# Layer A's tail in a two-layer decoder step on one core: which queue position the reload casts, the last head's output chain and a mixing of rows get

## The chip, the core and the metric

One core of a Trainium2 chip runs the whole step. The time is device microseconds of that core; smaller is better. TensorE does the matmuls, VectorE (DVE), ScalarE (ACT) and GpSimd (POOL) the elementwise work, and SyncE (SP) issues the DMAs.

## The reference

The input is 1024 prompt tokens and 8 sample tokens, 1032 columns in all, with model width 1024 and inner width 2048. Layer A is a gated linear recurrence in 8 heads, layer B a causal spatial gating unit. Both end in the same way:

```python
o = rmsnorm(o, g_norm).reshape(B, L, D_INNER)      # layer A, per head
y = (o * silu(z)) @ w_out
h = h + y
gate = sigmoid(rmsnorm(h, norm_ple[i]) @ w_ple_gate[i])
h = h + gate * (p[i] @ w_ple_proj[i])
```

The change touches the last head of layer A, the start of `w_out` in layer A, and one step of `w_out` in both layers.

## The kernel before, in words

**Layout.** Activations lie feature-major: 128 features on the partitions, tokens along the free dimension. The columns are cut into three groups c = 0, 1, 2 of 384, 384 and 264. A float32 product is made of three matmuls on rounded parts: `hi` is a ScalarE cast to the fast format, `lo` a DVE subtraction of what the cast lost (helper `split`; `bh`/`bl` are such pairs for activations, `whi`/`wlo` for weights).

**Order.** TensorE's program order is written out by hand: a tick counter runs small generators between the matmul groups, and each generator yields the number of ticks that it waits. The other engines' order is set by a scheduler from priorities (`tc.high_priority`), from `tc.issue_after(x)` (not ahead of x) and from when the code issues the work. At run time each engine works through its row strictly in order, so an instruction that waits holds up all that stands behind it. All DMAs here go through SP's one row.

**End of layer A.** For the last head (h = 7), `head_proj` makes the projections f, q, v and at last z (function `zz`, in the order c = 2, 0, 1). `recur` then works through eight tiles of 128 tokens: `pd` and `po` in PSUM, a state update on DVE (`S`), `out_sum` on ScalarE (a copy `on<-po`, then a square that sums). `finish` scales `on`, waits some ticks, transposes it on TensorE into `pt_o` (one buffer with the tag "pt"), and DVE multiplies it with z into `oz`, which is spilled to the DRAM tensor `ozd`. Beside this, `reload` brings the finished heads of `ozd` back as the `w_out` operand: for c = 0 through `zstg`, for c = 1 through three buffers `f`, row by row (DMA `f<-ozd`, cast `bh<-f`, subtraction `bl<-f,bh`). A buffer can be loaded again only when its subtraction is done.

**`last_fill`.** Between the last heads' steps TensorE runs twelve blocks of the per-layer embedding product (`pple`, PSUM tile `ps_pple`, three banks, each freed by a ScalarE copy to `pple_t`). Then come the first `w_out` products `ps_o`, which for c = 0 and 1 start before the loop over heads is drained. Rows of c = 2 are reloaded by `zstg<-ozd` into tiles that hold the `pple` operand until then (`bh_138`).

**`w_out`.** `out_phase` uses a seven-product form with sums of rows (`t1` to `t4`; function `unit`). It loads sums and residual rows (`raw<-d0t`, `h<-d0t`, `h<-in_xT`), and mixes two more sets of four rows for the second half: `quarters` loads them, `mix_rows` makes four DVE subtractions (`raw<-raw`), `store_sums` stores them. The hooks of `unit` (numbers after each product) say where that is issued. `exchange` reloads the results for the second half in the last unit of the first half.

Of the kernel before, what the change touches and what calls it, by code (L numbers as in the profile page):

```python
# [12 lines left out]
AF = mybir.ActivationFunctionType  # L13
# [12 lines left out]
NH = 8  # L26
# [4 lines left out]
PRI = 400  # L31
NWARM = 12
ZQ = 7
ZR = 3
# [7 lines left out]
W = (384, 384, 264)  # L42
# [38 lines left out]
def trunk_kernel(ctx, tc, xT, st, pT, nrm, wina, lbl, gna, wouta, winb, lng, lnb, lngr, lnbr,  # L81
# [3 lines left out]
    V, A, G, PE = nc.vector, nc.scalar, nc.gpsimd, nc.tensor  # L85
# [134 lines left out]
    last, rest = {}, {}  # L220
# [118 lines left out]
    def pple(l, ph, pl, half, place):  # L339

        wh, wl = take("p", l, half)
        for c in CH:
            for mm in range(4):
                ps = pp.tile([P, 512], F32, name="ps_pple", tag="mm", bufs=3)
                for k in range(2):
                    b = 2 * mm + k
                    mm3(ps[:, :W[c]], blk(wh, b), blk(wl, b), ph[c][:, k, :], pl[c][:, k, :], k == 0, k == 1)
                t = place(c, mm)
                with tc.high_priority(offset=PRI if l else 0):
                    last["pple"] = A.copy(t, ps[:, :W[c]])  # L350
                nc.sync.dma_start(ppd[l][4 * half + mm][:, OFF[c]:OFF[c] + W[c]], t)
                yield 1

# [1 line left out]
        nc.sync.dma_start(stg, src)  # L355
        split(hi, lo, stg)

    def load_zt(zt, parts, stage, n=2, lag=0, tie=True):


        todo = [(ozd[c][:, k0 + k:k0 + k + n, :], *(x[:, k:k + n, :] for x in zt[c, k0][:2]), W[c])
                for c, k0 in parts for k in range(0, zt[c, k0][2], n)]
        return load_list(todo, stage, lag, tie)

    def load_list(todo, stage, lag=0, tie=True, behind=False):

        stg = []
        def fetch(i):
            if i < len(todo):
                stg.append(stage(todo[i][3]))  # L370
                last["zt"] = nc.sync.dma_start(stg[i], todo[i][0])

        for i in range(len(todo) + lag):
            if not lag:
                fetch(i)
            if i >= lag:
                _, zh, zl, _ = todo[i - lag]
                with tc.issue_after(rest["u2"].ins) if behind else ExitStack():
                    hi = A.copy(zh, stg[i - lag])
                if tie:  # L380
                    tc.keep_in_program_order(hi)
                with tc.issue_after(rest["sum"].ins) if behind else ExitStack():
                    V.tensor_tensor(zl, stg[i - lag], zh.bitcast(F32), ALU.subtract)

            if lag:
                fetch(i)
            yield
# [258 lines left out]
    def z_gate(out, src, m, w, sg=None):  # L646
        sg = sg or fq.tile([P, 384], F32, name="sg", bufs=2)
        last["read"] = A.activation(sg[:, :w], src, AF.Sigmoid)
        V.scalar_tensor_tensor(sg[:, :w] if out is None else out, src, gn16[:, m:m + 1], sg[:, :w], ALU.mult, ALU.mult)
        return sg  # L650
# [46 lines left out]
    def head_proj(h, r):  # L697

        r["t0"] = tk.now
        if h:  # L700
            wt = take("a", 8 + h)
            for c in CH:
                fk(h, r, wt, c)
            wt = take("a", h)
            for c in CH:
                qq(h, r, wt, c)
                tk.spawn(decay(h, r, c), DEC[c])
        else:
            for c in CH:
                tk.spawn(decay(h, r, c), (1, 8, 18)[c])  # L710
        r["vs"] = wa.tile([NS, DV], F32, name="vs", bufs=1)
        tk.spawn(sample(h, r), 1)
        tk.spawn(recur(h, r), 1)
        for m in range(2):
            wt = take("a", 16 + 2 * h + m)
            for c in CH:
                w = W[c]
                ps = proj(wt, hh[c], hl[c], c)
                vf = wa.tile([P, 384], F32, name="vf", bufs=2)
                with tc.high_priority(offset=PRI):  # L720
                    last["read"] = A.copy(vf[:, :w], ps[:, :w])
                tk.spawn(v_token_major(h, r, m, c, vf), 3)
                tk.tick()
        if h < NH - 1:
            return

        def zz(wt, m, c):
            if not m:
                r["zs"][c] = wa.tile([P, 2, W[c]], F32, name=f"zs{c}")
            ps = proj(wt, hh[c], hl[c], c)  # L730
            z_gate(r["zs"][c][:, m, :], ps[:, :W[c]], m, W[c])
            tk.tick()
            if m == 1:
                r[f"z{c}"] = True

        wz, wz1 = take("a", 32 + 2 * h), take("a", 33 + 2 * h)
        zt.update(new_zt())
        for c in (2, 0, 1):
            zz(wz, 0, c)
            zz(wz1, 1, c)  # L740
            if c == 2:
                for cc in (0, 1):
                    tk.spawn(reload(r, cc))
                r["p"] = p_in_act(0, lambda w: wa.tile([P, 384], F32, name="vf", bufs=2)[:, :w])

    def reload(r, c):

        yield lambda: not any(p[2].__name__ == "mix_more" for p in tk.procs)
        lag = 2 + c
        gen = load_zt(zt, [(c, 0)], (stage2(wa, 2), one(lambda: fq.tile([P, 384], F32, name="f", bufs=3)))[c],  # L750
                      2 - c, lag, False)
        for _ in range(lag):
            next(gen)
        yield lambda: r.get(f"z{c}")
        for _ in gen:
            yield 1

    def v_token_major(h, r, m, c, vf):
        if not m:
# [122 lines left out]
    def out_sum(po, ss):  # L882

        on = wa.tile([P, DV], F32, name="on", bufs=6)
        with tc.high_priority(offset=PRI):
            A.copy(on, po)
            A.activation(po, po, AF.Square, accum_out=ss)
        return on

    def out_scale(ss, n):  # L890
# [45 lines left out]
    def finish(h, r, c, ss, ons):  # L936

        n = NT[c]
        if h < NH - 1:
            r["zs"][c] = wa.tile([P, 2, W[c]], F32, name=f"zs{c}")  # L940
            nc.sync.dma_start(r["zs"][c], zd[h][c])
            r[f"z{c}"] = True
        y = out_scale(ss[:, :n], n)
        yield 2
        with tc.issue_after(last["read"].ins):
            for i in range(n):
                A.activation(ons[i], ons[i], AF.Copy, scale=y[:, i:i + 1])
        yield (3, 3, 7)[c]
        yield lambda: r.get(f"z{c}") and slot(r, 2)
        oz = r["oz"][c] = wa.tile([P, 2, 384], F32, name="oz", bufs=2)  # L950
        for i in range(n):
            pt = out_transpose(ons[i], "pt")
            with tc.high_priority(offset=PRI):
                V.tensor_tensor(oz[:, :, i * P:(i + 1) * P], pt, r["zs"][c][:, :, i * P:(i + 1) * P], ALU.mult)
            yield 4 if i < n - 1 else 1
        if c < 2:
            spill(h, r, c)
            spilled.add((h, c))
# [69 lines left out]
    zt = {}  # L1028
    spilled = set()
    fine[0] = True  # L1030
    for h in range(NH):
# [5 lines left out]
        r = new_head() if h else r0  # L1037
# [52 lines left out]
    def out_phase(key, b, ssq, first, done, pre, begin):  # L1090
# [3 lines left out]
        with ExitStack() as s:  # L1094
# [117 lines left out]
            gen = [None]  # L1212
# [7 lines left out]
            def rows_of(m):  # L1220
                def go():
                    for i in (2, 3):
                        load_h(m + i)
                return go

            def exchange():

                assert next(mixer, None) is None
                o = dict(b)
                for n, to in (("b11", "b11"), ("b21", "t2"), ("b12", "b21"), ("b22", "t1"),  # L1230
                              ("t2", "t3"), ("t1", "b22"), ("t3", "t4"), ("t4", "b21")):
                    b[n] = o[to]
                todo = quarter("b11") + quarter("b21") + quarter("b12") + quarter("b22")
                todo += [(ozd[2][:, 8 + k, :], b["c2"][0][:, k, :], b["c2"][1][:, k, :], W[2]) for k in range(8)]
                todo += quarter("t2") + quarter("t1") + quarter("t3") + quarter("t4")
                turns = itertools.cycle([zr] * ZR + [lambda w: raw()[:, :w]] * 4)
                gen[0] = load_list(todo, lambda w: next(turns)(w), ZR + 4, False, True)
                steps(gen[0], ZR + 4)()

            def last_exchange():  # L1240
# [2 lines left out]
                steps(gen[0], ZR)()  # L1243

            units(0, range(2, KT, 2), {2: (rows_of(2), {5: mix1}),
                                       4: (rows_of(4), {2: mix1}),
                                       KT - 2: (exchange, {2: jobs(4), 3: jobs(4), 5: jobs(6), 7: jobs(6)})})
            for m in range(2):
                wt = take(key, m, 1)
                for c in CH:  # L1250
                    ps = plain(bank(), wt, c)
# [167 lines left out]
    for q in range(0, 4, 2):  # L1419
        wv = take("b", MI + q), take("b", MI + q + 1)  # L1420
        for c in CH:
            for m in range(2):
                ps = proj(wv[m], hh[c], hl[c], c)
# [137 lines left out]
    for g in range(8):  # L1561
# [18 lines left out]
        else:  # L1580

            zt = {(0, 0): (hh[0], hl[0], 8), (1, 0): (*xm[1], 4), (1, 4): (*xm[0], 4), (2, 0): (hh[2], hl[2], 8)}
# [161 lines left out]
```

## Time and profile before

| what | value |
|---|---|
| runs | 1866.89 us median (1864.61 to 1870.77, 3 runs) |
| the profiled execution's own time | 1863.58 us |
| its span | 1861.6 us, mean granted clock 0.995 |
| busy share of the span | TensorE 98%, DVE 73%, ScalarE 48%, GpSimd 22% |
| chain that ended last | TensorE 80%, DVE 10%, DMA 5% |

The kernel is bound by TensorE nearly everywhere. What is not matmul time lies in single waits of about a microsecond, the longest in the stretch from 700 to 800 us, where layer A ends and its `w_out` begins. To read it: a timeline's row gives the start, the duration, the engine, the line and the tiles; square brackets give the idle time ahead of it and who ended that.

### The profile page before, as it was taken

The page shows a single profiled execution, that of the slowest core. Times are in us where ns is not written, and L with a number is a line of the kernel's source. Part 1 is how long each engine was busy: PE and PEld are TensorE (multiplying, and loading weights), DVE is VectorE, ACT ScalarE, POOL GpSimd, SP SyncE. Part 2 cuts the span into 40 slices and gives each one's busy share as a digit, 9 for nine tenths or more (in the row PEclk, how much of TensorE's full clock was granted, in tenths as well). Part 3 has the DMA queues.
Part 4 walks back from the last instruction along what each step waited for, and adds up shares of the span by engine and source line. Part 5 has one row for each costly group of instructions (what it writes and reads, how often), then busy time and mean ns, then how long its engine had stood idle before and what let it go on. Part 6 is the DMA issues. An engine that isn't in the chain of part 4 may idle for free.

```text
span 1861.6 us, 37133 instructions
## 1 busy us (share of the span) xinstructions
PE 1822.4 (98%) x14458; PEld 1788.6 (96%) x14458; DVE 1360.5 (73%) x2760; ACT 897.6 (48%) x1905; POOL 402.3 (22%) x407
## 2 busy tenths in 40 slices
PE   8999999999999999999999999999999999999997
PEld 7999999999999998999999999999999999999997
DVE  7766888889888875867756755577778877877744
ACT  7533366556656655344444544434443435444342
POOL 4000011111111110000323233354444552000222
PEclk9999999999999999999999999999999999999999
DMA  6233344345444355853244343323334546953223
GB/s 220 79 112 106 112 127 128 108 152 182 149 130 140 117 176 185 278 184 96 87 145 140 101 136 92 95 79 119 129 117 143 172 129 215 305 179 104 72 92 114
DMA packets 164560, 258.11 MB, mean 139 GB/s; under 512 B 16096, under 2 KB 136864, under 8 KB 163360
## 3 DMA queue, kind: packets, MB, share of 16 engines
q1 hardware_dynamic: 164384, 255.74, 43.5%
q8 instruction: 113, 1.85, 0.4%
q14 instruction: 63, 0.52, 0.1%
HBM read 182.88 MB, written 72.80 MB: 137 GB/s over the span
## 4 chain that ended last, share of the span: by engine, by line
PE 80%; DVE 10%; DMA 5%; issue 2%; POOL 1%; ACT 1%; SPq 0%; DVEq 0%; ACTq 0%; POOLq 0%
PE ps_proj L228 19%; PE ps_proj L230 18%; PE ps_proj L229 18%; PE ps_d L228 2%; PE ps_o L228 2%; PE ps_d L230 2%; PE ps_d L229 2%; PE ps_o L229 2%; PE ps_o L230 2%; DVE wlo L150 1%; PE psp L1526 1%; DMA vb<-vd 1%; PE pt_o L899 1%; PE pt_g L1408 1%; PE pC L807 1%
## 5 line engine op out<-in xcount | busy, mean ns | idle before, releaser
L228 PE MATMUL ps_proj<-bh,whi 128*128 128x264 f32 (+1 forms) x2248 | 719.2, 320 | 4.3 <-ACT u L493 1.3
L229 PE MATMUL ps_proj<-bl,whi 128*128 128x264 f32 (+1 forms) x2248 | 700.8, 312 | 5.4 <-DVE bl L224 2.7
L230 PE MATMUL ps_proj<-bh,wlo 128*128 128x264 f32 (+1 forms) x2248 | 700.9, 312 | 1.2 <-DVE wlo L150 1.2
L228 PEld LDWEIGHTS ps_proj<-bh,whi 128*128 128x128 f32 x2248 | 423.6, 188 | 12.3 <-issue 3.3
L229 PEld LDWEIGHTS ps_proj<-bl,whi 128*128 128x128 f32 x2248 | 424.1, 189 | 8.9 <-DVE bl L224 5.4
L230 PEld LDWEIGHTS ps_proj<-bh,wlo 128*128 128x128 f32 x2248 | 422.6, 188 | 2.1 <-DVE wlo L150 2.1
L150 DVE TENSOR_TENSOR wlo<-wstg,whi 128x1024 fp32r<-128x1024 f32 x148 | 183.7, 1241 | 109.4 <-ACT whi L149 109.1
L149 ACT CAST whi<-wstg 128x1024 fp32r<-128x1024 f32 x148 | 155.2, 1049 | 150.0 <-PE ps_proj L229 125.0
L149 ACT CAST shi<-ssum 128x512 fp32r<-128x512 f32 x152 | 94.1, 621 | 187.3 <-PE ps_proj L229 90.1
L150 DVE TENSOR_TENSOR slo<-ssum,shi 128x512 fp32r<-128x512 f32 x152 | 113.9, 751 | 9.2 <-ACT shi L149 8.8
L237 POOL TENSOR_TENSOR rsq<-rms_e,mhalf 128x3 f32<-128x3 f32 x15 | 17.8, 1187 | 368.1 <-DVE rms_e L282 368.1
L857 DVE TENSOR_TENSOR qk<-qk,t 128x384 f32<-128x384 f32 (+1 forms) x144 | 77.2, 540 | 12.0 <-PE pC L807 11.3
L228 PE MATMUL ps_proj<-xmh,shi 128*128 128x384 f32 x244 | 83.0, 340 | 1.9 <-ACT xmh L223 1.7
L229 PE MATMUL ps_proj<-xml,shi 128*128 128x384 f32 x244 | 81.9, 336 | 0.7 <-DVE xml L224 0.7
L230 PE MATMUL ps_proj<-xmh,slo 128*128 128x384 f32 x244 | 81.7, 335 | 0.0
L228 PE MATMUL ps_o<-bh,whi 128*128 128x384 f32 (+1 forms) x232 | 73.4, 316 | 0.0
L230 PE MATMUL ps_o<-bh,wlo 128*128 128x384 f32 (+1 forms) x232 | 72.7, 313 | 0.0
L229 PE MATMUL ps_o<-bl,whi 128*128 128x384 f32 (+1 forms) x232 | 72.7, 313 | 0.0
L1535 POOL TENSOR_TENSOR s<-s,u 128x384 f32<-128x384 f32 (+1 forms) x48 | 54.1, 1127 | 70.9 <-DVE s L1529 70.3
L1274 DVE TENSOR_TENSOR tmp<-tmp,pj 128x384 f32<-128x384 f32 (+1 forms) x48 | 25.6, 534 | 55.9 <-ACT tmp L1273 52.0
L237 POOL TENSOR_TENSOR rsq<-ss_e,mhalf 128x3 f32<-128x3 f32 (+2 forms) x32 | 28.4, 889 | 145.7 <-DVE ss_e L893 145.7
L264 POOL TENSOR_TENSOR ssq<-ssq,tmp 128x384 f32<-128x384 f32 (+1 forms) x36 | 34.3, 951 | 108.1 <-ACT tmp L263 108.1
(376 smaller groups left out, 4135.8 us busy)
## 6 DMA issues: line engine op xcount, KB each, us to landing
wstg<-in_wina SPq DMA_DIRECT2D x48, 512.0 KB, 3.8
wstg<-in_winb SPq DMA_DIRECT2D x48, 512.0 KB, 4.0
pj<-ppd SPq DMA_DIRECT2D x16, 516.0 KB, 4.9
S<-in_st SPq DMA_DIRECT2D x16, 512.0 KB, 5.4
vb<-vd SPq DMA_DIRECT2D x16, 512.0 KB, 4.8
out_so_s<-S SPq DMA_DIRECT2D x16, 512.0 KB, 3.5
wstg<-in_wouta SPq DMA_DIRECT2D x16, 512.0 KB, 4.2
wstg<-in_wgate SPq DMA_DIRECT2D x16, 512.0 KB, 3.7
```

The source lines that it names most:

```text
L149: A.copy(hi, src)
L150: V.tensor_tensor(lo, src, hi.bitcast(F32), ALU.subtract)
L228: PE.matmul(ps, wh, xh, start=first, stop=False, skip_group_check=more)
L229: PE.matmul(ps, wh, xl, start=False, stop=False, skip_group_check=more)
L230: PE.matmul(ps, wl, xh, start=False, stop=last, skip_group_check=more)
L237: G.tensor_tensor(y, e, mhalf[:, :n], ALU.pow)
L264: eng.tensor_tensor(ssq, ssq, sq[:, :w], ALU.add)
L807: PE.matmul(out(slice(row, row + kt.shape[1])), kt, qt, start=True, stop=True)
L857: V.tensor_tensor(lev, lev, t2.rearrange("p two (n o) -> p two n o", o=1).broadcast_to([P, 2, n, lv]), ALU.mult)
L899: PE.transpose(pt[:, m, :], on[:, m * P:(m + 1) * P], ident)
L1274: V.tensor_tensor(gt[:, :w], gt[:, :w], pj[:, OFF[c]:OFF[c] + w], ALU.mult)
L1535: G.tensor_tensor(s[:, :w], s[:, :w], us[mm, c][:, :w], ALU.mult)
```

## The change

1. `pple` and `out_sum` note their last ScalarE instruction as `last["out"]`; `reload` for c = 1 hands it to `load_list`, so that each cast of a reloaded row is put behind the last such copy or square. `load_list`'s argument `behind` becomes a function for that. The first two of these rows and every second one after them keep a pause of one tick, the others get two.
2. In `finish`, the last head waits 2 ticks ahead of its transposes in place of 3, 3 and 7.
3. The gate of the last head's z gets the higher priority.
4. In both `out_phase`s the last set of rows is mixed after product 5 of unit 4, not after product 2.

```diff
                 with tc.high_priority(offset=PRI if l else 0):
-                    last["pple"] = A.copy(t, ps[:, :W[c]])
+                    last["out"] = last["pple"] = A.copy(t, ps[:, :W[c]])
...
-    def load_list(todo, stage, lag=0, tie=True, behind=False):
+    def load_list(todo, stage, lag=0, tie=True, behind=None):
...
-                with tc.issue_after(rest["u2"].ins) if behind else ExitStack():
+                first = behind and behind()
+                with tc.issue_after(first.ins) if first else ExitStack():
                     hi = A.copy(zh, stg[i - lag])
                 if tie:
                     tc.keep_in_program_order(hi)
-                with tc.issue_after(rest["sum"].ins) if behind else ExitStack():
+                with tc.issue_after(rest["sum"].ins) if first and "sum" in rest else ExitStack():
                     V.tensor_tensor(zl, stg[i - lag], zh.bitcast(F32), ALU.subtract)
...
             ps = proj(wt, hh[c], hl[c], c)
-            z_gate(r["zs"][c][:, m, :], ps[:, :W[c]], m, W[c])
+            with tc.high_priority(offset=PRI):
+                z_gate(r["zs"][c][:, m, :], ps[:, :W[c]], m, W[c])
...
         gen = load_zt(zt, [(c, 0)], (stage2(wa, 2), one(lambda: fq.tile([P, 384], F32, name="f", bufs=3)))[c],
-                      2 - c, lag, False)
+                      2 - c, lag, False, lambda: last["out"] if c else None)
...
-        for _ in gen:
-            yield 1
+        for i, _ in enumerate(gen):
+            yield 1 if i < 2 or i % 2 or not c else 2
...
-            A.activation(po, po, AF.Square, accum_out=ss)
+            last["out"] = A.activation(po, po, AF.Square, accum_out=ss)
...
-        yield (3, 3, 7)[c]
+        yield (3, 3, 7)[c] if h < NH - 1 else 2
...
-                gen[0] = load_list(todo, lambda w: next(turns)(w), ZR + 4, False, True)
+                gen[0] = load_list(todo, lambda w: next(turns)(w), ZR + 4, False, lambda: rest["u2"])
...
-                                       4: (rows_of(4), {2: mix1}),
+                                       4: (rows_of(4), {5: mix1}),
```

The rows of POOL and everything ahead of the last head's final tiles are the same in both programs. Three places differ.

**Place 1, the last head's transposes.** On DVE before, from the state update of the last tile on (`oz_10161` is c = 0, `oz_10318` c = 1):

```order
L924 SCALAR_TENSOR_TENSOR S_10290<-S_10229,t128_10058,pd_10279 128x256
L383 TENSOR_TENSOR bl1_140<-f_10298,bh1_137 128x384
L383 TENSOR_TENSOR bl1_140<-f_10316,bh1_137 128x384
L383 TENSOR_TENSOR bl1_140<-f_10335,bh1_137 128x384
L954 TENSOR_TENSOR oz_10161<-pt_o_10310,zs0_9951 128x2x128
L893 TENSOR_SCALAR ss_e2_10337<-ss_10217 128x2
L954 TENSOR_TENSOR oz_10318<-pt_o_10319,zs1_10123 128x2x128
```

And now, up to the third tile of c = 1:

```order
L926 SCALAR_TENSOR_TENSOR S_10290<-S_10229,t128_10058,pd_10279 128x256
L956 TENSOR_TENSOR oz_10161<-pt_o_10310,zs0_9951 128x2x128
L956 TENSOR_TENSOR oz_10318<-pt_o_10319,zs1_10123 128x2x128
L895 TENSOR_SCALAR ss_e2_10337<-ss_10217 128x2
L384 TENSOR_TENSOR bl1_140<-f_9987,bh1_137 128x384
L384 TENSOR_TENSOR bl1_140<-f_9989,bh1_137 128x384
L384 TENSOR_TENSOR bl1_140<-f_9991,bh1_137 128x384
L384 TENSOR_TENSOR bl1_140<-f_10298,bh1_137 128x384
L956 TENSOR_TENSOR oz_10318<-pt_o_10380,zs1_10123 128x2x128
L384 TENSOR_TENSOR bl1_140<-f_10316,bh1_137 128x384
L384 TENSOR_TENSOR bl2_141<-zstg_10467,bh2_138 128x528
L150 TENSOR_TENSOR wlo_10405<-wstg_10267,whi_10404 128x1024
L956 TENSOR_TENSOR oz_10318<-pt_o_10431,zs1_10123 128x2x128
```

The two `oz` now stand ahead of the subtractions; the third tile's `oz` of c = 1 stands behind two of them, one of c = 2 and a weight's `wlo`. On ScalarE the casts of that stretch now stand between the copies:

```order
L888 COPY on_10293<-po_10280 128x256
L889 ACTIVATE po_10280,ss_10217<-po_10280 128x256
L380 CAST bh1_137<-f_9987 128x384
L380 CAST bh1_137<-f_9989 128x384
L949 ACTIVATE on_10235<-on_10235,rsq2_10339 128x256
L350 COPY pple_t_10307<-ps_pple_10323 128x384
L380 CAST bh1_137<-f_9991 128x384
L949 ACTIVATE on_10293<-on_10293,rsq2_10339 128x256
L350 COPY pple_t_10348<-ps_pple_10341 128x384
L350 COPY pple_t_10358<-ps_pple_10351 128x384
L380 CAST bh1_137<-f_10298 128x384
L350 COPY pple_t_10358<-ps_pple_10367 128x384
```

Before, six of the eight casts stood ahead of the second copy. The row goes on with `f_10316`, a copy, the cast of `zstg_10467`, a copy, and the weight's cast `whi_10404`. On TensorE, between the tenth and eleventh block, there were the transposes of one tile before, and now there are those of two tiles in a row (c = 1's third, c = 2's first):

```order
L230 MATMUL ps_pple_10421<-bh2_138,wlo_9758 128x264
L901 MATMUL pt_o_10431<-ident_68,on_10148 128x128 x2
L901 MATMUL pt_o_10436<-ident_68,on_10235 128x128 x2
L228 MATMUL ps_pple_10440<-bh2_138,whi_9757 128x264
L229 MATMUL ps_pple_10440<-bl2_141,whi_9757 128x264
```

**Place 2, SP's row ahead of `w_out`.** Before, from a copy's store to the first load of sums:

```order
L962 DMA ozd1_74<-oz_10318 128x768
L189 DMA wstg_10673<-in_wouta 128x1024
L351 DMA ppd0_7_83<-pple_t_10444 128x264
L371 DMA zstg_10469<-ozd2_75 128x2x264
L962 DMA ozd2_75<-oz_10504 128x2x264
L189 DMA wstg3_10818<-in_wouta 128x1024
L1320 DMA raw_10606<-d0t1_117 128x384
```

Now:

```order
L964 DMA ozd1_74<-oz_10318 128x768
L351 DMA ppd0_7_83<-pple_t_10447 128x264
L371 DMA zstg_10479<-ozd2_75 128x2x264
L189 DMA wstg_10673<-in_wouta 128x1024
L964 DMA ozd2_75<-oz_10435 128x2x264
L189 DMA wstg3_10818<-in_wouta 128x1024
L1322 DMA raw_10606<-d0t1_117 128x384
```

The last rows of c = 2 (`zstg`) come ahead of a weight, and on DVE `oz` of c = 2's last tile now stands ahead of the subtraction of those rows, where it stood behind it. The loads behind it are the same, with the weight `wstg_11028` behind `h<-d0t` of rows 6 and 7 rather than ahead of them, and `wstg_10819` ahead of four more loads.

**Place 3, the mixing in unit 4 of `w_out`.** On DVE before:

```order
L426 TENSOR_TENSOR raw_10992<-raw_10994,raw_10992 128x384
L1150 TENSOR_TENSOR h2_4_10590<-h2_4_10590,ps_proj_11118 128x264
L427 TENSOR_TENSOR raw_10994<-raw_10994,raw_10991 128x384
L150 TENSOR_TENSOR wlo_11033<-wstg_11028,whi_11032 128x1024
L509 TENSOR_TENSOR u4_11157<-ps_proj_11144,u2_11081 128x384
L150 TENSOR_TENSOR slo_11044<-ssum_11036,shi_11043 128x512
L428 TENSOR_TENSOR raw_10993<-raw_10993,raw_10994 128x384
L201 TENSOR_TENSOR ssum_11036<-wstg_11028,ssum_11036 128x512
L516 TENSOR_TENSOR c22_11172<-ps_d_11159,u4_11157 128x384
```

Now the four stand behind the sum `c22`:

```order
L517 TENSOR_TENSOR c22_11164<-ps_d_11151,u4_11149 128x384
L150 TENSOR_TENSOR slo_11050<-ssum_11047,shi_11049 128x512
L426 TENSOR_TENSOR raw_10991<-raw_10992,raw_10991 128x384
L1152 TENSOR_TENSOR h1_5_10583<-h1_5_10583,c22_11164 128x384
L427 TENSOR_TENSOR raw_10992<-raw_10994,raw_10992 128x384
L524 TENSOR_TENSOR u4_11149<-ps_proj_11175,u4_11149 128x384
L150 TENSOR_TENSOR slo_11055<-ssum_11036,shi_11054 128x512
L428 TENSOR_TENSOR raw_10994<-raw_10994,raw_10991 128x384
L1152 TENSOR_TENSOR h1_4_10582<-h1_4_10582,u4_11149 128x384
L530 TENSOR_TENSOR u2_11081<-ps_d_11151,u2_11081 128x384
L429 TENSOR_TENSOR raw_10993<-raw_10993,raw_10994 128x384
```

The same move stands in layer B's `w_out`.

More of the change, by code (lines that the diff above doesn't have):

```diff
@@ L356, in load_split, with load_zt @@
         split(hi, lo, stg)
-    def load_zt(zt, parts, stage, n=2, lag=0, tie=True):
+    def load_zt(zt, parts, stage, n=2, lag=0, tie=True, behind=None):
         todo = [(ozd[c][:, k0 + k:k0 + k + n, :], *(x[:, k:k + n, :] for x in zt[c, k0][:2]), W[c])
                 for c, k0 in parts for k in range(0, zt[c, k0][2], n)]
-        return load_list(todo, stage, lag, tie)
-    def load_list(todo, stage, lag=0, tie=True, behind=False):
+        return load_list(todo, stage, lag, tie, behind)
+    def load_list(todo, stage, lag=0, tie=True, behind=None):
         stg = []
```

## The prediction

> **What bounds the kernel now.** First the page, for the busy shares.
>
> ```profile
> PE 1822.4 (98%) x14458; PEld 1788.6 (96%) x14458; DVE 1360.5 (73%) x2760; ACT 897.6 (48%) x1905; POOL 402.3 (22%) x407
> ```
>
> TensorE is the bound, so only its idle time and its slow time can be won. Next the waits of TensorE between 640 and 820 us, where the change lies (total, times, longest):
>
> ```profile
> PE pt_o L899 <- DVE oz L954: 4.2, 1, 4.2
> PE ps_proj L228 <- ACT xmh L223: 1.7, 1, 1.7
> PE ps_proj L228 <- DVE zs L649: 1.2, 1, 1.2
> PE ps_d L228 <- DVE c L516: 1.1, 1, 1.1
> PE ps_proj L229 <- DVE xml L224: 0.7, 2, 0.5
> ```
>
> Then stretches of 10 us, for the granted clock (the number after POOL):
>
> ```profile
> 720.00:730.00 10.00, 7.86 (x31) 7.83 (x32) 3.85 (x9) 5.76 (x15) 0.70 (x1) 0.66 0.44 157
> 760.00:770.00 10.00, 7.56 (x41) 6.66 (x40) 8.53 (x18) 5.05 (x10) 0.00 (x0) 0.96 1.00 339
> 770.00:780.00 10.00, 10.00 (x59) 10.00 (x59) 5.49 (x10) 2.29 (x3) 0.00 (x0) 0.87 0.69 238
> ```
>
> Two of the waits are followed by a lower clock, 0.66 and 0.87, so they cost more than their idle time. The wait for `zs` lies at 685, ahead of the first row that differs: nothing is won there.
>
> **Term 1, the last head's transposes.** TensorE's timeline:
>
> ```profile
> 717.52 0.38 PE L899 MATMUL pt_o<-ident,on 128*128 128x128 f32 x2
> 722.14 0.69 PE L899 MATMUL pt_o<-ident,on 128*128 128x128 f32 x2 [4.24 <-DVE oz L954]
> 722.48 0.67 PE L228 MATMUL ps_pple<-bh,whi 128*128 128x384 f32 x1
> 728.32 0.33 PE L228 MATMUL ps_pple<-bh,whi 128*128 128x384 f32 x1
> 728.50 0.33 PE L229 MATMUL ps_pple<-bl,whi 128*128 128x384 f32 x1
> 734.82 0.34 PE L228 MATMUL ps_o<-bh,whi 128*128 128x384 f32 x1
> ```
>
> From 722.48 to 728.32 there are 18 matmuls; at the pitch of the two rows behind, 0.175, they would take 3.1 us: 2.7 lost to the clock. The cause is read from DVE and ScalarE:
>
> ```profile
> 720.16 1.59 DVE L383 TENSOR_TENSOR bl<-f,bh 128x384 fp32r<-128x384 f32 x3 [2.19 <-ACT bh L379]
> 721.66 0.42 DVE L954 TENSOR_TENSOR oz<-pt_o,zs 128x256 f32<-128x256 f32 x1
> 719.61 1.54 ACT L379 CAST bh<-f 128x384 fp32r<-128x384 f32 x3 [2.46 <-DMA f<-ozd]
> 721.06 0.47 ACT L350 COPY pple_t<-ps_pple 128x384 f32<-128x384 f32 x1
> ```
>
> The one `pt_o` buffer waits for `oz`, which stands behind three subtractions, they behind three casts, they behind a DMA. In the new row both `oz` stand ahead of them. Transposes (0.38) plus `oz` (0.42) plus two hand-overs of 0.06 (721.66 + 0.42 to 722.14) put the second pair at 717.52 + 0.92 = 718.4: 0.5 of idle time remains, 3.7 goes. With it I let the clock's 2.7 go too.
>
> What is late next? The casts now stand between the copies that free the three `ps_pple` banks. TensorE at full pitch (a block is six matmuls, 1.05; a narrow one, 264 columns for 384, 0.73) gets from 718.4 over six blocks and two transposes to the new pair of transposes at 726.4. The second of that pair waits for c = 1's third `oz`, hence for `wlo`, hence for `whi`, behind casts of rows that are reloaded late. Row 4 can be fetched when row 1 is subtracted, about 719.9. These rows price the landing and the work:
>
> ```profile
> DMA to landing us min/median/max: 2.4/3.3/3.5
> 731.38 0.63 ACT L379 CAST bh<-zstg 128x528 fp32r<-128x528 f32 x1
> 732.32 1.05 ACT L149 CAST whi<-wstg 128x1024 fp32r<-128x1024 f32 x1
> 733.40 1.23 DVE L150 TENSOR_TENSOR wlo<-wstg,whi 128x1024 fp32r<-128x1024 f32 x1 [0.65 <-ACT whi L149]
> ```
>
> The first row is that of tile `f`. 719.9 + 3.3 is 723.2; from there ScalarE has two casts of rows (0.5 each), three copies (0.45), one cast of `zstg` (0.6) and `whi` (1.05): 727.2. `wlo` ends at 728.4, `oz` at 728.8, and TensorE goes on at 728.9 after some 2.0 us of idle time. Two narrow blocks and the sample's transposes later, `ps_o` starts at 730.6 instead of 734.82: **4.2 us**. From above, without the new wait, it is 6.2. From below, a new wait as long as the old with the same loss of clock (another 2.2 + 2.7) leaves -0.7. I take 4.2: a wait near 2 us did not lower the clock elsewhere,
>
> ```profile
> 218.83 0.25 PE L807 MATMUL pC<-qk 128*32 128x64 f32 x3 [1.82 <-DVE qk L857]
> 215.00:220.00 5.00, 3.18 (x109) 2.81 (x107) 5.00 (x14) 1.02 (x2) 0.00 (x0) 1.00 0.14 25
> ```
>
> where the clock is 1.00 in that stretch. Shorter pauses of `finish`, the z gate's priority and the moved transposes add no instruction; their cost is the new wait.
>
> **Term 2, the loads of `w_out`.** The wait for `xmh` and those for `xml` beside it:
>
> ```profile
> 764.87 0.44 PE L229 MATMUL ps_proj<-xml,shi 128*128 128x384 f32 x1 [0.54 <-DVE xml L224]
> 767.23 0.44 PE L228 MATMUL ps_proj<-xmh,shi 128*128 128x384 f32 x1 [1.75 <-ACT xmh L223]
> 769.42 0.52 PE L228 MATMUL ps_proj<-bh,whi 128*128 128x384 f32 x1
> 772.64 0.28 PE L228 MATMUL ps_proj<-bh,whi 128*128 128x264 f32 x1
> 737.80 0.33 SPq L189 DMA_DIRECT2D wstg<-in_wouta  x1
> 738.77 0.44 SPq L371 DMA_DIRECT2D zstg<-ozd  x1
> 746.08 0.37 SPq L962 DMA_DIRECT2D ozd<-oz  x1
> 760.80 2.18 SPq L1320 DMA_DIRECT2D h<-d0t  x4
> 744.87 0.71 DVE L383 TENSOR_TENSOR bl<-zstg,bh 128x528 fp32r<-128x528 f32 x1 [5.03 <-ACT bh L379]
> 745.64 0.42 DVE L954 TENSOR_TENSOR oz<-pt_o,zs 128x256 f32<-128x256 f32 x1
> ```
>
> Idle time is 1.75 + 0.7 = 2.4. The slow matmuls, from 769.1 to 772.64 (7 wide, 6 narrow), take 3.5 us and would take 7 x 0.175 + 6 x 0.12 = 2.0: together **4.0 us**. They wait for sums whose DMAs SP could not issue ahead of the spill at 746.08. That waited for `oz`, which stood behind a subtraction that waited for the `zstg` load of 738.77, and that load stood behind a weight's. In the new rows `zstg` passes the weight and `oz` passes the subtraction. `oz` is then due when TensorE transposes the last tile halfway between `ps_o` of c = 0 and c = 1, 4.2 us behind 730.6, at about 735.3: the spill goes some 10.5 us earlier, while TensorE is only 4.2 ahead. The next gate on SP, a weight's buffer, hangs on a `whi` and `wlo` that follow TensorE's `ps_o` of c = 2 (730.6 + 2 x 4.2 + 2.9 = 741.9). So the rest is issued from 744.2 on, 13 loads at some 0.5 us: the last at 750.5, where the last four of sums went at 760.8 and later, 10 us earlier against TensorE's 4.2. I take all 4.0. From below: if TensorE arrives 4.2 earlier and the sums don't, the wait grows by that, -4.2.
>
> [...]
>
> **Term 3, the mixing in unit 4.**
>
> ```profile
> 794.68 0.56 DVE L426 TENSOR_TENSOR raw<-raw 128x384 f32<-128x384 f32 x1 [3.98 <-DMA raw<-ozd]
> 799.84 0.44 PE L228 MATMUL ps_d<-bh,whi 128*128 128x384 f32 x1 [1.10 <-DVE c L516]
> 800.60 0.32 SPq L371 DMA_DIRECT2D raw<-ozd  x1
> 812.17 1.34 ACT L379 CAST xmh<-raw 128x384 fp32r<-128x384 f32 x3
> ```
>
> DVE waits 4 us for a DMA with TensorE's sums behind it, and three more subtractions of about 0.5 stand ahead of `c`. Put behind `c`, they hold up no sum that is late, and their data has landed by then: **1.1 us** are won. The mixing ends some 5 us later, and its four stores (SP) and the four `raw` loads behind them move with it. The last load goes from 800.6 to about 805.5, lands near 809, and its cast is due at 813: hidden, as is the weight's load that now passes these stores. Layer B has no wait of TensorE at this place, so 0 there; either could be from -1.1, if a subtraction delays a sum as much as before, to the 1.1.
>
> **Sum.** 4.2 + 4.0 + 1.1 = 9.3 us. The profiled execution took 1863.58, so it would be 1854.3. The runs shown have their median at 1866.89, 3.3 above that execution; against it the time is **1857.6**, and this I predict.
>
> **Rivals.** (a) *The wait only moves*: row 4 lands late, the new pair of transposes waits over 3 us and the clock falls again. For it: the chain over DMA, two casts, `whi` and `wlo` is as long as the one removed. Against: both ends of it were priced above. Term 1 is -0.7, the rest holds: 4.4, so 1862.5, which a measurement cannot tell from no change (I take 0.3%, 5.6 us, as that bound). (b) *The loads stay late* for another reason, such as the sA buffers that they reuse or the full DMA share (1.00 at 760 to 770): term 2 is 0, the gain 5.3, 1861.6. (c) *Slower*: casts that wait for DMA stand between the copies, so each late landing holds up TensorE's banks. Rows 4 to 8 come in three generations, each fetched after a subtraction of the one ahead. With x us beyond 3.3 each, the last ones cost 3x and the clock 2.7: 9.3 - 2.7 - 3x. All reads of `ozd` in the trace:
>
> ```profile
> DMA to landing us min/median/max: 1.8/3.2/5.3
> ```
>
> At the longest, x = 2, 0.6 is still won; it becomes slower by 0.3% from x = 4.1, where the time is 1872.5. (d) *It does nothing*: the DVE row shows that the order did change, and all three terms would have to fail.
>
> **How the numbers follow.** The forecast holds 0.68, (a) 0.12, (b) 0.13, (c) 0.04, (d) 0.03. Faster by over 0.3% takes the forecast's share and a little of (b): 0.72; slower (c) and some of (d): 0.05; within: 0.23. The likeliest case alone reaches from a gain of 6.5 to one of 11.3 (term 1 at its top), 1855.6 to 1860.4. For 8 in 10 I go below by the scatter of the runs (2.3 under their median) and above to (a): 1852.5 to 1863.5.
>
> **What would show it.** Right: `pt_o`'s wait of 4.24 becomes one near 0.5, a wait near 2 us on DVE's `oz` stands between the tenth and eleventh `pple` block, the clock is 1.00 from 720 to 780, the spill `ozd<-oz` of c = 2 is issued near 735, no wait for `xmh` or `xml` is left, `ps_d` no longer waits for `c` in unit 4. Wrong: a slow clock behind the new pair, `ps_pple` waiting for `pple_t`, or TensorE still waiting for `xmh`.

## The result, and the profile after

| | before | after |
|---|---|---|
| median of 6 runs | 1867.76 us (1861.58 to 1871.06) | 1856.04 us (1854.45 to 1857.85) |
| profiled execution, its span | 1863.58, 1861.6 | 1854.45, 1852.4 |

The ratio of the runs is 0.9941, with a 95% interval of 0.9925 to 0.9958: the changed kernel is faster by 11 us (8 to 14). 1857.6 was predicted.

The page's busy shares, where TensorE has the same 14458 matmuls in 5.2 us less of busy time (1822.4 before), mostly because slow ones have gone (in before 9.5 us of the busy time, 6.09 + 3.40, lie at a clock of 0.50; rows in the last section):

```profile
PE 1817.2 (98%) x14458; PEld 1784.3 (96%) x14458; DVE 1364.2 (74%) x2760; ACT 896.1 (48%) x1905; POOL 403.7 (22%) x407
```

TensorE's waits between 640 and 840 us (total, times, longest), all that are left:

```profile
PE pt_o L901 <- DVE oz L956: 2.0, 2, 1.5
PE ps_proj L228 <- DVE zs L650: 1.2, 1, 1.2
PE pos L1000 <- DVE zs L650: 0.7, 1, 0.7
PE ps_proj L228 <- ACT vf L722: 0.2, 1, 0.2
```

The waits for `xmh`, `xml` and, in this stretch, for `c` are gone; that of `pos` is new. The three stretches that were shown of before (granted clock behind the five busy times), all at 1.00 now:

```profile
720.00:730.00 10.00, 8.51 (x56) 8.23 (x55) 6.00 (x12) 8.20 (x19) 0.94 (x1) 1.00 0.86 289
760.00:770.00 10.00, 10.00 (x67) 10.00 (x66) 6.49 (x12) 2.29 (x3) 0.00 (x0) 1.00 1.04 363
770.00:780.00 10.00, 10.00 (x60) 10.00 (x59) 9.74 (x18) 3.40 (x5) 0.00 (x0) 1.00 0.73 245
```

To see where the time came from, the stretch that the change can touch is cut in three, by first starts in TensorE's timeline. Before:

```profile
641.14 0.38 PE L899 MATMUL pt_o<-ident,on 128*128 128x128 f32 x2
776.95 0.33 PE L228 MATMUL ps_d<-xmh,shi 128*128 128x384 f32 x1
827.40 0.33 PE L228 MATMUL ps_o<-xmh,whi 128*128 128x384 f32 x1
```

and after:

```profile
641.60 0.38 PE L901 MATMUL pt_o<-ident,on 128*128 128x128 f32 x2
731.43 0.42 PE L228 MATMUL ps_o<-bh,whi 128*128 128x384 f32 x1
768.33 0.33 PE L228 MATMUL ps_d<-xmh,shi 128*128 128x384 f32 x1
817.39 0.34 PE L228 MATMUL ps_o<-xmh,whi 128*128 128x384 f32 x1
```

The first `ps_o` of before stands in the prediction (734.82). Stage 1 runs from the first `pt_o` in this stretch, ahead of all that differs, to the first `ps_o`; stage 2 from there to the first `ps_d`; stage 3 to the first `ps_o` on `xmh`.

| us | stage 1 | stage 2 | stage 3 | sum |
|---|---|---|---|---|
| before | 93.68 | 42.13 | 50.45 | 186.26 |
| after | 89.83 | 36.90 | 49.06 | 175.79 |
| won | 3.85 | 5.23 | 1.39 | 10.47 |
| predicted (terms 1, 2, 3) | 4.2 | 4.0 | 1.1 | 9.3 |

What lies around these stages scatters. In the 14 profiles of this study the first `pt_o` comes between 640.85 and 644.21 though the program up to there is the same, and from the last anchor to the end of the span it takes 1032.9 to 1036.7. So the two profiled executions differ by 9.1, not by 10.5, and the medians by 11.7; only the stages are compared below where a microsecond matters.

### The profile page after: what moved, and what is told of

The parts are those of the page before. It is cut to its first block, busy times and chain, and to the rows that moved or that the text cites. A ratio compares the mean times of both kernels' runs of the same rounds, so it can differ in the third digit from the quotient of the medians.

```text
span 1852.4 us, 37136 instructions
## 1 busy us (share of the span) xinstructions
PE 1817.2 (98%) x14458; PEld 1784.3 (96%) x14458; DVE 1364.2 (74%) x2760; ACT 896.1 (48%) x1905; POOL 403.7 (22%) x407
## 4 chain that ended last, share of the span: by engine, by line
PE 81%; DVE 10%; DMA 5%; issue 2%; POOL 1%; ACT 1%; SPq 0%; DVEq 0%; POOLq 0%; ACTq 0%
PE ps_proj L228 19%; PE ps_proj L230 19%; PE ps_proj L229 19%; PE ps_d L228 3%; PE ps_d L230 3%; PE ps_d L229 3%; PE ps_o L228 2%; PE ps_o L230 2%; PE ps_o L229 2%; DMA vb<-vd 1%; PE psp L1528 1%; DVE wlo L150 1%; PE pt_o L901 1%; PE pt_g L1410 1%; DVE bl L224 1%
```

## The experiments

Twelve kernels; the time of each is compared with runs of the kernel before in the same session (medians there: 1866.74, 1868.05 and 1867.13 for the three groups of four). The stages are read from each kernel's one profile, as above.

| kernel | median us | ratio to before, 95% | stage 1 | stage 2 | stage 3 | sum |
|---|---|---|---|---|---|---|
| e1 only casts | 1860.84 | 0.9966 (0.9954 to 0.9978) | 87.10 | 41.89 | 49.91 | 178.90 |
| e2 only head | 1864.38 | 0.9984 (0.9974 to 0.9994) | 94.50 | 36.92 | 49.05 | 180.47 |
| e3 only mix | 1864.42 | 0.9986 (0.9977 to 0.9995) | 93.33 | 43.15 | 49.06 | 185.54 |
| e4 only z | 1865.62 | 0.9995 (0.9986 to 1.0003) | 93.63 | 42.99 | 50.05 | 186.67 |
| e5 no casts | 1859.28 | 0.9953 (0.9940 to 0.9965) | 95.39 | 36.92 | 49.06 | 181.37 |
| e6 no head | 1858.25 | 0.9955 (0.9941 to 0.9968) | 87.10 | 42.49 | 49.06 | 178.65 |
| e7 no mix | 1857.06 | 0.9943 (0.9930 to 0.9955) | 89.03 | 36.90 | 49.39 | 175.32 |
| e8 no z | 1855.60 | 0.9933 (0.9921 to 0.9946) | 89.03 | 36.93 | 49.06 | 175.02 |
| e9 even c = 1 | 1853.48 | 0.9922 (0.9910 to 0.9935) | 87.43 | 37.45 | 49.06 | 173.94 |
| e10 even all | 1851.02 | 0.9915 (0.9901 to 0.9928) | 87.54 | 36.93 | 49.06 | 173.53 |
| e11 fill 6 | 1867.08 | 0.9997 (0.9988 to 1.0006) | 92.88 | 42.74 | 50.55 | 186.17 |
| e12 fill 12 | 1871.04 | 1.0020 (1.0009 to 1.0030) | 96.50 | 42.91 | 50.46 | 189.87 |

The columns repeat: stage 1 is 87 to 90 with the casts moved and 93 to 96.5 without, stage 2 is 36.9 to 37.5 with the shorter head and 42 to 43 without. That is most of the answer. The details follow.

**One part alone, on the kernel before.**

e1, the casts and the pauses between them (no run parts the two):

```diff
-        for _ in gen:
-            yield 1
+        for i, _ in enumerate(gen):
+            yield 1 if i < 2 or i % 2 or not c else 2
...
-                      2 - c, lag, False)
+                      2 - c, lag, False, lambda: last["out"] if c else None)
```

> The kernel before with the casts of reloaded rows put behind ScalarE's copies, and nothing else of the change. My theory (three separate steps, of which this part carries only the first wait): pt_o's wait of 4.24 becomes about 0.5 and the clock stays at 1.00 from 720 to 730, so TensorE reaches the first ps_o some 5 us earlier; but oz of the sample columns still stands behind the subtractions of zstg, the spill still goes near 745, and TensorE, now earlier, waits for xmh and xml by what it won, in place of 2.4 some 6 us. Net 0 to -1.5 us against before. Rival (the casts carry all of it): the waits for xmh and xml go too, and the time falls by 8 to 11 us, as with the whole change. Rival (each part brings its own term, whatever the others do): -4 to -6 us, with the wait for xmh staying at 2.4.

Measured: faster by 6.3 us (4.1 to 8.6). Its three annotated waits on TensorE from 715 to 775 us:

```profile
718.65 0.44 PE L900 MATMUL pt_o<-ident,on 128*128 128x128 f32 x2 [0.52 <-DVE oz L955]
758.80 0.44 PE L229 MATMUL ps_proj<-xml,shi 128*128 128x384 f32 x1 [0.58 <-DVE xml L224]
761.01 0.46 PE L228 MATMUL ps_proj<-xmh,shi 128*128 128x384 f32 x1 [1.60 <-ACT xmh L223]
```

The first wait behaves as expected, 4.24 to 0.52. The rest of my expectation fell: the waits for the sums did not grow by what TensorE won; they stayed at 2.2 (2.4 before). The rival that each part brings its own term held. The reason is on SP, in e1's rows:

```profile
738.73 0.37 SPq L963 DMA_DIRECT2D ozd<-oz  x1
739.66 1.86 SPq L1321 DMA_DIRECT2D raw<-d0t  x4
754.69 1.76 SPq L1321 DMA_DIRECT2D h<-d0t  x3
```

The spill went at 746.08 before, the last group of these loads at 760.80. Both came 6 to 7 us earlier without being touched: they hang on `oz` and on weights' buffers that follow TensorE, so they move with it.

e2, the head's pause:

```diff
-        yield (3, 3, 7)[c]
+        yield (3, 3, 7)[c] if h < NH - 1 else 2
```

> The kernel before with the shorter pause of the last head's finish, and nothing else. My theory: the wait of 4.24 for oz at the first pair and its 2.7 us of slow clock stay; oz of the sample columns now stands ahead of the subtractions of zstg, the spill goes near 738, so the waits for xmh and xml (2.4) and the slow matmuls behind them (1.5) go: -4.0 us, less up to 1.5 for the wait between the two pairs of transposes that now follow each other, so -2.5 to -4. Rival (this part carries all): -8 to -11 us. Rival (the sums are late for another reason, the buffers they reuse or the DMA share of 1.00 there): 0 to +2 us, with a wait for xmh still there.

Measured: faster by 3.0 us (1.1 to 4.9), in the expected range; its stages give 5.8, which lies outside that interval. In its profile the clock falls once more behind the stages, from 1571 to 1575 (see the last section), which hides some of it; the rest is open. Its waits on TensorE in that stretch are the old long one and the new one, and none for sums:

```profile
722.35 0.69 PE L900 MATMUL pt_o<-ident,on 128*128 128x128 f32 x2 [3.36 <-DVE oz L955]
735.06 0.44 PE L900 MATMUL pt_o<-ident,on 128*128 128x128 f32 x2 [1.49 <-DVE oz L955]
```

Stage 2 falls to 36.92, stage 1 rises by 0.8. So term 2 belongs to the head part alone.

e3, the mixing:

```diff
-                                       4: (rows_of(4), {2: mix1}),
+                                       4: (rows_of(4), {5: mix1}),
```

> The kernel before with the second mixing of quarters in unit 4 of w_out put from the second to the fifth place, and nothing else. My theory: ps_d no longer waits for c (1.10 in before) and the time falls by 1.1 us, so the ratio to before is 0.9994, which may be lost in the scatter; the trace decides. Rival: the wait only moves to another tile, 0 us.

Measured: 2.6 us (0.9 to 4.3); stage 3 falls by 1.39 and the wait for `c` is gone. The larger figure of the times has the stage's within its interval; the sum of the three stages fell by only 0.7, as stage 2 came out 1.0 longer.

e4, the z gate:

```diff
-            z_gate(r["zs"][c][:, m, :], ps[:, :W[c]], m, W[c])
+            with tc.high_priority(offset=PRI):
+                z_gate(r["zs"][c][:, m, :], ps[:, :W[c]], m, W[c])
```

> The kernel before with the z gate of the last head at high priority, and nothing else. My theory: it wins nothing (0 to +0.7 us): the wait of 1.2 for zs at 685 stays, and a wait of about 0.7 of pos for zs (near 707), which the changed kernel has and the kernel before has not, comes with this part, since the gate now stands ahead of the state's update on VectorE. Rival: oz and the transposes of the last head depend on zs, so the earlier gate shortens pt_o's wait of 4.24 by the gate's 0.5 to 1 us, and the time falls by as much.

Measured: no difference outside the interval (-2.6 to +0.6 us). It does have the wait of `pos` (0.88), and its long wait of `pt_o` is shorter (3.6), but stage 1 as a whole is where it was (93.63). That this wait comes from the gate, as I expected, is not borne out: see e8.

**One part undone, on the changed kernel** (each the reverse of the diff above).

> The changed kernel without the part on the casts (they stand in ScalarE's queue where they stood before). My theory: the wait for oz at the first pair of transposes (4.24 in before) and the 0.66 clock behind it are back, so the first ps_o is 4 to 5 us later than in the changed kernel; the spill of the sample columns is still early, so no wait for xmh or xml: +4 to +5 us against the changed kernel, -5 to -7 against before. Rival (the shorter chain of the last head is enough, the casts matter little): within 1 us of the changed kernel.

> The changed kernel with the long pause of the last head's finish. My theory: the first pair's wait stays gone and so does the new one between the two pairs (1.49), so the first ps_o is up to 1.5 us earlier than in the changed kernel; but the spill goes after the subtractions of zstg again, and TensorE waits for xmh and xml by 4 to 8 us with a lower clock behind: +4 to +6 us against the changed kernel, -4 to -6 against before. Rival (the sums are early because the weights' loads were passed, not because of the spill): no wait for xmh, and the time 1 us below the changed kernel.

> The changed kernel with the second mixing of quarters at its old place in unit 4. My theory: ps_d waits for c there again, about 1.1 us, and the time is 1.1 us above the changed kernel. Rival (a): 0, since the earlier stores let the rows land earlier and the subtractions no longer stand in the way. Rival (b): more than 2 us, since TensorE now arrives 8 us earlier and the rows do not.

> The changed kernel without the z gate's priority. My theory: the wait of pos for zs (0.72 at 707) is gone and nothing takes its place, so -0.7 us against the changed kernel. Rival: the gate comes later and oz of the last head with it; the wait between the pairs of transposes grows from 1.49 by the gate's 0.5 to 1 us: +0 to +0.5.

e5: stage 1 is back at 95.39, 5.6 above the changed kernel, with waits of 3.55 and 1.49 and a clock of 0.66 from 720 to 730. The shorter head is not enough, and the rival falls. Against before it is 8.8 us faster (6.5 to 11.2), more than I expected and more than the 4.9 of its stages; the stages come from one profile and leave the rest open.

e6: stage 1 is 2.7 better than in the changed kernel and stage 2 5.6 worse, as TensorE waits for sums again:

```profile
760.76 0.44 PE L228 MATMUL ps_proj<-xmh,shi 128*128 128x384 f32 x1 [2.48 <-ACT xmh L223]
```

In sum 2.9 worse in the stages and 2.6 in the times (0.9955 against 0.9941), where I expected 4 to 6. The loss behind `ps_o` was of the expected size, though the waits make up only 2.8 of it (2.48, 0.18 and 0.15) where I expected 4 to 8; the rest is slow matmuls behind them (starts 0.32 apart from 762.22 to 765.10, in place of 0.175). The gain of stage 1 was expected at 1.5 at most; of its 2.7, 0.7 is the wait of `pos`, which e6's profile does not have. What e6's SP does, and the changed kernel's:

```profile
749.79 2.32 SPq L1322 DMA_DIRECT2D h<-d0t  x5
753.59 0.33 SPq L189 DMA_DIRECT2D wstg<-in_wouta  x1
753.97 2.28 SPq L1322 DMA_DIRECT2D h<-d0t  x3
```

```profile
747.65 0.33 SPq L189 DMA_DIRECT2D wstg<-in_wouta  x1
750.41 3.88 SPq L1322 DMA_DIRECT2D h<-d0t  x8
```

In e6 a weight's load that must wait for its buffer stands between the fifth and the sixth of the eight loads, in the changed kernel ahead of all. The head part moves that as well, so the spill's time (737.63 in e6, 736.56 after) is only part of the mechanism.

e7: stage 3 is 49.39, 0.33 above the changed kernel, with no wait for `c` there. Rival (a) held: once the other parts are in, the mixing's place is worth 0.3, not 1.1. e2 and e5 say the same of kernels without the casts (49.05 without the move, 49.06 with it). The terms 2 and 3 are not independent.

e8: stage 1 is 0.80 better, the wait of `pos` is gone, and the times are 1.5 us lower within intervals that overlap. The number is the expected one, but its cause is not shown: e7, which keeps the priority and is the changed kernel up to there, has the same stage 1 (89.03) and no wait of `pos`, and e10, which has no such priority, waits there. After, then e7, then e10:

```profile
702.37 0.88 DVE L992 SCALAR_TENSOR_TENSOR S<-vb,qs,S 128x256 f32<-128x256 f32 x2 [3.38 <-DMA vb<-vd]
707.72 1.07 PE L1000 MATMUL pos<-S,qm 128*32 128x256 f32 x16 [0.72 <-DVE zs L650]
```

```profile
702.25 0.88 DVE L992 SCALAR_TENSOR_TENSOR S<-vb,qs,S 128x256 f32<-128x256 f32 x2 [2.12 <-DMA vb<-vd]
708.09 1.07 PE L1000 MATMUL pos<-S,qm 128*32 128x256 f32 x16
```

```profile
703.18 0.88 DVE L991 SCALAR_TENSOR_TENSOR S<-vb,qs,S 128x256 f32<-128x256 f32 x2 [3.22 <-DMA vb<-vd]
708.34 1.07 PE L999 MATMUL pos<-S,qm 128*32 128x256 f32 x16 [0.72 <-DVE kl L224]
```

Where `pos` waits, it takes 5.35 from the landing of `vb` to `pos` with the gate ahead of `kl` (after) and 5.16 with it behind (e10). So the priority costs 0.2, and only where the row lands late. Of all 14 profiles `pos` waits in six, three with the priority (after, e4, e5) and three without (e10, e11, e12); counted from the start of stage 1 the row lands at 60.7 us or later in these six, and at 60.3 or earlier in the other eight. The wait is scatter of that landing and not the gate's.

**Taking away the new wait.** On the changed kernel without the z gate's priority, e9 has a pause of 2 between the last head's transposes of c = 1, e10 one of 3 for all:

```diff
-            yield 4 if i < n - 1 else 1
+            yield (4 if h < NH - 1 else (4, 2, 4)[c]) if i < n - 1 else 1     # e9
+            yield (4 if h < NH - 1 else 3) if i < n - 1 else 1                # e10
```

> The changed kernel without the z gate's priority and with a pause of 2 in place of 4 between the last head's transposes of c = 1, so that no pair of them follows another without a block between, but for the first two. My theory: the wait of 1.49 for oz behind wlo goes, since the third oz of c = 1 now stands ahead of wlo, and the spill of the sample columns stays near 735: -1.5 us against the same kernel with pauses of 4 (the run without the z gate's priority), with no waits for xmh or xml. Rival: the wait is due to wlo and moves to the next oz behind it (0 us), as it moved from the first pair to this one.

> The same with pauses of 3 for all of the last head's transposes: no two pairs follow each other at all. My theory: the first wait of 0.52 goes too, so -2.0 us against the run without the z gate's priority. Rival: a fourth oz stands behind wlo, which waits for whi, and 0.5 to 1.5 us of wait come back there, 0 to -1 us.

e9's one wait of `pt_o`, of two in the changed kernel; e10 has none, its only wait from 700 to 840 us being that of `pos`:

```profile
718.18 0.44 PE L900 MATMUL pt_o<-ident,on 128*128 128x128 f32 x2 [0.52 <-DVE oz L955]
```

```profile
PE pos L999 <- DVE kl L224: 0.7, 1, 0.7
```

Against e8 the stages give 1.1 for e9 (1.6 in stage 1; 0.5 lost in stage 2, mostly in gaps of a tenth of a microsecond near 739.7 and 758.5) and 1.5 for e10 (2.2 without its wait of `pos`); the ratios to before give 2.1 and 3.4, with intervals that overlap e8's. Both rivals fall. The medians of the two, from one session, lie 2.5 apart where the stages give 0.4; that e10 is ahead is shown by both, by how much is not. e10 is the fastest kernel of the study: 1851.02 us, 0.9915 of before (0.9901 to 0.9928), with a median 5.0 us under that of the changed kernel, which was timed in another session.

**What lowers the clock.** On the kernel before, the block of `pple` ahead of the long wait is done twice (e11) or three times (e12), where each repetition starts its sums anew.

```diff
-                for k in range(2):
+                for k in (0, 1) * (3 if (l, half, c, mm) == (0, 1, 0, 1) else 1):     # e11: 2
```

> The kernel before, with the six matmuls of the ple block ahead of the long wait done twice (the second time gives the same sums): 1.05 us of extra work just ahead of the wait of 4.24. The wait is ended by VectorE, so it shrinks to about 3.2 and TensorE goes on at the same time. My theory (a gap of 2.5 already lowered the clock elsewhere, so one of 3.2 does too): the slow pitch of 0.32 is still there behind it, 0 us against before. [...]

> The kernel before, with the six matmuls of that block done three times: 2.1 us of extra work, and a wait of about 2.1. My theory (what lowers the clock is the idle time within a few us; one gap of 1.8 did not lower it, gaps of 2.2 in sum did): at the edge; if the clock holds, the slow matmuls go and the time falls by 2.6 us with more work done; if not, 0. Rival (the slow matmuls belong to the start after the transposes, not to the idle time): slow pitch unchanged, 0 to +0.5 us.

e11's wait, and the rows between which eleven matmuls follow each other at a slow pitch, up to 0.33:

```profile
723.20 0.44 PE L899 MATMUL pt_o<-ident,on 128*128 128x128 f32 x2 [2.91 <-DVE oz L954]
724.53 0.45 PE L228 MATMUL ps_pple<-bh,whi 128*128 128x384 f32 x1
727.98 0.36 PE L230 MATMUL ps_pple<-bh,wlo 128*128 128x384 f32 x1
```

A gap of 2.91 lowered the clock, and 1.05 us of extra work cost nothing, as my theory had it; the slow matmuls were eleven in place of eighteen. The gap lies between two pairs of transposes; from the `ps_pple` matmul ahead of them (719.73 + 0.34) to the next at 723.39 it is 3.3 us. The gap of 2.48 in e6 has no transposes beside it.

e12 missed both expectations. The wait did not shrink:

```profile
726.45 0.69 PE L899 MATMUL pt_o<-ident,on 128*128 128x128 f32 x2 [4.74 <-DVE oz L954]
725.50 0.56 DVE L383 TENSOR_TENSOR bl<-f,bh 128x384 fp32r<-128x384 f32 x1 [1.89 <-ACT bh L379]
725.98 0.42 DVE L954 TENSOR_TENSOR oz<-pt_o,zs 128x256 f32<-128x256 f32 x1
```

A longer block ahead of it moved `oz` behind a fourth subtraction, which waits for the next landing. So it is 3.9 us slower (1.7 to 5.6), and says nothing of a gap of 2.1. It shows once more what term 1 removes: `oz` behind a subtraction, that behind a cast, that behind a DMA.

## Why the prediction was right, and where its steps were not

**Term 1** (4.2 predicted, 3.85 measured) came out by its steps. In the changed kernel:

```profile
718.54 0.38 PE L901 MATMUL pt_o<-ident,on 128*128 128x128 f32 x2
719.44 0.44 PE L901 MATMUL pt_o<-ident,on 128*128 128x128 f32 x2 [0.52 <-DVE oz L956]
726.85 1.05 ACT L149 CAST whi<-wstg 128x1024 fp32r<-128x1024 f32 x1
727.93 1.22 DVE L150 TENSOR_TENSOR wlo<-wstg,whi 128x1024 fp32r<-128x1024 f32 x1 [0.65 <-ACT whi L149]
729.07 0.42 DVE L956 TENSOR_TENSOR oz<-pt_o,zs 128x256 f32<-128x256 f32 x1
729.55 0.44 PE L901 MATMUL pt_o<-ident,on 128*128 128x128 f32 x2 [1.49 <-DVE oz L956]
```

The old wait is 0.52, as worked out. The new one is where it was expected, behind `whi`, `wlo` and `oz`, and 1.49 where 2.0 were taken: that chain ended 0.65 later than priced (729.55 for 728.9), TensorE came 1.3 later (the pair ahead at 727.68 for 726.4). It kept the clock, and did so in all five profiles that have a wait of 1.49 there (after, e2, e5, e7, e8). That the clock would hold at the 2.0 of the forecast was less sure than it looked: the prediction's evidence was a wait of 1.82 in before, and the same wait, of 1.80, has a clock of 0.66 behind it in e5 (rows in the last section). So there was some luck in letting the clock's 2.7 go. (The text of the term counts six blocks up to the new pair; the sum has eight, 6 x 1.05 + 2 x 0.73.) From the pair at 717.52 (718.54) to `ps_o` it won 17.30 - 12.89 = 4.4; 0.56 were lost ahead of that pair, by the wait of `pos` (0.72). The prediction had no such wait; it priced the z gate's priority at nothing, which is right to 0.2, and the rest is the scatter of `vb`'s landing (see e8).

**Term 2** (4.0 predicted, 5.23 measured) was right in its cause and too small. From the first `ps_proj` on `xmh` to the first `ps_d` the time went from 762.94:776.95 to 759.18:768.33, 14.01 to 9.15, so 4.9. Idle time is 2.4 of that. For the slow matmuls I counted 1.5; most of the other 0.9 lies at and right behind the three waits, where starts are 0.28 to 0.44 apart after the idle time is taken off, in place of 0.175. Ahead of that first `ps_proj` a further 0.37 was won, where before had two pairs of transposes behind `ps_o` and the changed kernel has one: I charged that pair to term 1 and did not credit it here. The times of the step were off by more: the spill went at 736.56 for 735.3, and the last of the sums' loads at 754.29 for 750.5, since the weight's gate opened at 747.65 and not at 744.2. TensorE needed them from 759.18 on, so this cost nothing.

The bound below, that the wait grows by what TensorE wins (-4.2), was the wrong mechanism. e1 shows it: TensorE 6 us earlier, the wait unchanged, because the loads came earlier with it (spill 7.4, last group 6.1); they hang on buffers that follow TensorE.

**Term 3** (1.1 predicted, 1.39 measured in e3) was right as a change of the kernel before, but not as a term of its own beside term 2: with the head part in, the mixing is worth 0.3 (e7). The sum is not hurt by this, since the wait goes once and the stage shows 1.39, whichever part takes it away. In e7 DVE still waits 3.28 for those rows (3.98 in before) and TensorE no longer waits for `c`; how the head part brings that about is left open. Layer B shows no gain, as said: its part of the span lies inside the scatter.

**Rivals.** (a) half happened, since the wait did move, but at 1.49 it kept the clock. (b) fell: no wait for a sum is left. (c) fell: there is no wait of `ps_pple` for a copy. (d) fell.

**The sum** of the stages is 1.2 above the forecast's 9.3, most of it the slow starts behind the waits of term 2. Each term is off by less than the 3 us or so by which the stretches around the stages scatter, and the misses of the terms (-0.35, +1.23, +0.29) partly cancel. The lower end of the likeliest case, a gain of 6.5, is not worked out in the prediction. The time of 1856.04 is 1.6 below the forecast, with the median before at 1867.76, 0.9 above the one that it was made against.

## What to carry to other kernels

When an in-order queue makes a short instruction wait behind work that hangs on a DMA (here `oz` of 0.42 us, for which TensorE waited 4.24), move the instruction ahead and then price the next thing in that queue: the wait that takes its place (here `wlo` between two transposes, 1.49) can be found in the order beforehand, and other pauses between the transposes (e9, e10) removed it. Test terms in both directions, alone and undone, since two that remove the same wait add up only once. Before charging "TensorE arrives earlier than its data", ask what frees the data's buffer: if that is TensorE itself, the data moves with it (in e1 TensorE came 6 us earlier and the loads 6.1 to 7.4).

## What the runs showed of the hardware

In before the granted clock falls to half twice in the stretch of the stages and comes back. The first fall lasts 6.82 us; the second comes 40.95 us after its end and lasts 3.40:

```profile
721.41:728.23 6.82, 6.09 (x20) 6.09 (x21) 2.38 (x6) 3.46 (x10) 0.70 (x1) 0.50 0.52 183
728.24:769.19 40.95, 38.51 (x252) 37.51 (x251) 26.70 (x48) 20.40 (x38) 0.00 (x0) 1.00 0.79 264
769.20:772.60 3.40, 3.40 (x14) 3.40 (x13) 2.27 (x5) 1.04 (x1) 0.00 (x0) 0.50 1.05 359
```

Falls stand behind single idle gaps of 2.91 us (e11, starts 0.32 apart behind it), 3.36 (e2, a clock of 0.66 from 720 to 730), 3.55 (e5, 0.66), 4.24 (before, 0.66) and 4.74 (e12, starts 0.32 apart), and behind groups of short ones within 4 us: 0.69, 1.60 and 0.15 in e11 (starts 0.32 apart from 769.22 to 772.10), 0.18, 2.48 and 0.15 in e6 (0.32 apart from 762.22), 0.54, 1.75 and 0.15 in before (a clock of 0.50 from 769.20). But in these runs the size of a gap does not settle it. The wait of `pC` that the prediction shows with the clock at 1.00 (1.82 in before) has a fall behind it in e5:

```profile
218.80 0.25 PE L809 MATMUL pC<-qk 128*32 128x64 f32 x3 [1.80 <-DVE qk L859]
220.00:225.00 5.00, 5.00 (x25) 4.93 (x22) 4.95 (x16) 3.23 (x8) 1.38 (x2) 0.66 0.22 83
```

In e2 the clock is 0.50 from 1571.23 to 1574.63, behind a wait of 1.43 for `pple_t`; before has that wait too (1.44) and stays at 1.00. Behind single gaps of 1.49 the clock held in five profiles of five. So a gap of 1.43 and one of 1.80 have a fall behind them, one of 1.44 and one of 1.82 have none, and these runs give no threshold.

A fall can begin ahead of the wait's end or behind it: 0.7 us ahead in before (721.41 against 722.14), 1.4 behind in e11 (724.60 against 723.20), 2.0 behind in before's second case (769.20 against 767.23). What sets its beginning is not shown.
